# Expert numbers sent later, gates in 8 KB rows, a later residual and 28 lead tiles in a Conformer-S5-PEER block

## The chip, the cores and the metric

The kernel runs on one core of a Trainium2 chip. The metric is the device time of one execution in microseconds; the time before is 3585.42 us, the median of three runs (3583.12 to 3587.71). Engines are named as the profile names them: PE (TensorE, matmuls), PEld (its weight loads), DVE (VectorE), ACT (ScalarE), POOL (GpSimd) and SP (SyncE, which here only issues DMAs).

## The reference

One decoder block over 512 tokens of width 2048, in float32. A convolution branch and a diagonal state-space branch are mixed by gates, projected by `w_out` and added to `x`. The change touches only what follows, the PEER layer:

```python
x = x + merged @ w_out[l]
h = rmsnorm(x, norm_ffn[l])
x = x + peer(h, ...)
return rmsnorm(x, norm_final)

def block(xb):                                   # 128 tokens
    q = (xb @ w_q).reshape(128, 8, 2, 128)
    s = einsum('thcd,hcnd->thcn', q, sub_keys)
    s_top, i_top = top_k(s, 16)                  # per half
    best, pos = top_k(all 256 sums of pairs, 16)
    expert = i_top[..., 0, i] * 128 + i_top[..., 1, j]   # of the pairs that won
    gates = softmax(best)
    act = gelu(einsum('td,thkd->thk', xb, u_tab[expert]))
    return einsum('thk,thkd->td', gates * act, v_tab[expert])
```

There are 128 x 128 = 16384 experts, each with a row of 2048 in `u_tab` and one in `v_tab`; each token uses 8 heads x 16 experts.

## The kernel before

**Three kinds of token.** The last 352 tokens (`ND`) are computed densely: all 16384 experts for all of them, with gates that are zero where an expert is not chosen. The first 128 tokens (block A) and the next 32 (block B) are computed by gathering the rows of the chosen experts by indirect DMAs: 128 rows of U and 128 of V for block A, 32 and 32 for block B (there one partition holds a quarter of a token's experts). A gathered row lands in a `row` tile, three of which exist (`NROW`), and one DVE instruction over 2048 elements takes it in (line 1011 for U, line 1022 for V).

**U tiles and V tiles.** The dense part is cut into 128 tiles of 128 experts. A U tile (`dense_u`, 48 matmuls) multiplies a 128 x 2048 piece of the U table with the normed tokens; GELU on ACT makes `ga` of it (line 862). `weigh` multiplies `ga` by the gates on POOL (line 1081) and splits the product in a high and a low part. A V tile (`dense_v`, 48 matmuls) takes four weighed tiles (a group, `GRP`) and a quarter of the width; its four PSUM results are added into `acc` by DVE (line 1135). There are 32 groups of four V tiles. Every weight piece of 128 x 1024 is loaded by SP (line 222, `wraw`), its high part cast by ACT (`whi`, line 204), its low part made by DVE or by POOL (`wlo`, line 205), because each product is made of three float32r matmuls.

**The lead.** The gates need the whole routing, so the first `LEAD` = 24 U tiles run before any V tile and park their `ga` in DRAM (`d_ga`). For the first `UPOOL` = 10 of them POOL makes both low parts, for the others DVE. After U tile `LAG` - 1 = 5, `transp_routes` makes the softmax (`gt`), spreads the gates of block B over the partitions, and transposes expert numbers and gates. From U tile 6 on, gate steps (`gate_prep`, `gate_tokens`) run between the matmuls: 88 steps of four tokens, each with two comparisons on DVE, a product on POOL (every third step) or ACT, four matmuls and two copies. Every eighth step ends with two DMAs of 1 MB that write `stg` to `d_g`. The last step falls `TAIL` = 2 tiles before the lead's end. From U tile 10 on, `pump_rows` adds `RLEAD` = 1.5 steps of the gathering per tile.

**V-only tiles, then the main loop.** In groups 0 to 4 the next group's four `ga` are reloaded from `d_ga`, so there is no U matmul, only V tiles; one gather step (`RV`) goes with each. `acc` starts as the residual, loaded from `d_x2` by four DMAs in group 0. From then on each iteration has a U tile and a V tile and `rate` gather steps, about 2.9.

**What sets the order.** The kernel is written for a planner, the Tile framework's. It estimates each instruction's duration, and whenever an engine is free by its estimate, that engine gets the instruction that is ready and stands first in the program. Place in the program is thus a priority. The queue that comes out is fixed when the program is built, and on the chip each engine works through its queue in order. `issue_after` (`after` in the code) ties an instruction behind another one on its engine. The gathers are tied behind POOL's latest split or product in that way (`pace`), the softmax's exponential behind the latest GELU. `spread`, which sends the expert numbers or gates of block B to DRAM (line 823) and reads them back in four pieces (line 825), all on POOL, is tied to nothing. Before the change it is called for the expert numbers at line 830, ahead of the first U tile.

Of the kernel before, what the change touches and what calls it, by code (L numbers as in the profile page):

```python
# [7 lines left out]
F32 = mybir.dt.float32  # L8
# [22 lines left out]
G0 = GA + GB  # L31
ND = T - G0
BLKS = [(0, 128), (128, 128), (256, 96)]
NE = 128
LEAD = 24
TAPS = 10
P1 = 2.8
P2 = 4.0
LAG = 6
GM = 1  # L40
TAIL = 2
NR = 18
NROW = 3
RLEAD = 1.5
RV = 1.0
UPOOL = 10
GRP = 4


def _mul(nc, o, a, b):  # L50
    nc.vector.tensor_tensor(o, a, b, op=ALU.mult)
# [6 lines left out]
def _add(nc, o, a, b):  # L58
    nc.vector.tensor_tensor(o, a, b, op=ALU.add)  # L59
# [94 lines left out]
def kernel(ctx, tc, xT, vecs, cst, w_in, conv_w_out, w_vg, w_out, w_q, keysT,  # L154
                      sprm, sb_ch, sb_st, sc_st, gffn, gfin, peer_u, peer_ut, peer_v, peer_vt, out):
    nc = tc.nc
    MS = bass.MemoryType
    const = ctx.enter_context(tc.tile_pool(name="const", bufs=1))
    dram = ctx.enter_context(tc.tile_pool(name="dram", bufs=1, space=MS.DRAM))
# [13 lines left out]
    d_x2 = dram.tile([KD, 128, T], F32, name="d_x2")  # L173
    d_p = dram.tile([4, 64, 64], F32, name="d_p")
    d_k = dram.tile([32, 32, 128], F32, name="d_k")
    d_g = dram.tile([ND // 32, NE // GRP, 128, GRP, 32], F32, name="d_g")
    d_eb = dram.tile([GB, 128], I32, name="d_eb")
    d_gb = dram.tile([GB, 128], F32, name="d_gb")
    d_ga = [dram.tile([128, ND], F32, name=f"d_ga{j}") for j in range(LEAD)]

# [59 lines left out]
    def proj(ps, srcs, ah, al, eng=None, side=0.0, mid=None):  # L240
        for _ in proj_steps(ps, srcs, ah, al, eng, side):
            if mid:
                mid()
# [48 lines left out]
    with tc.issue_after(last_x):  # L292
        for k in range(KD):
            p = k % 3 == 2
# [120 lines left out]
    acc = []  # L415
# [386 lines left out]
    def softmax():  # L802
        g = gt.rearrange("p b h k -> p (b h) k")
        with tc.issue_after(last_ga[0]):
            nc.scalar.activation(g, g, AF.Exp)
        nc.vector.tensor_reduce(zs, g, axis=AX.X, op=ALU.add)
        nc.vector.reciprocal(zs, zs)
        _mul(nc, g, g, zs[:, :, None].to_broadcast([128, TB * 8, 16]))

    eidx = con2.tile([128, HK], I32, name="eidx")  # L810
    eidb = con2.tile([128, GB], I32, name="eidb")
# [3 lines left out]
    def expert_ids(o, b):  # L815
        ef = tmp("ef")[:, :128]
        nc.vector.scalar_tensor_tensor(ef, ij[:, 0, b].rearrange("p h k -> p (h k)"), 128.0,
                                       ij[:, 1, b].rearrange("p h k -> p (h k)"), op0=ALU.mult, op1=ALU.add)
        nc.vector.tensor_copy(o, ef)

    def spread(o, d, src):

        nc.gpsimd.dma_start(d, src[:GB])
        for c in range(REP):
            nc.gpsimd.dma_start(o[c * GB:(c + 1) * GB, :], d[:, c * 32:(c + 1) * 32])

    eid1 = con2.tile([128, HK], I32, name="eid1")
    expert_ids(eidx, 0)
    expert_ids(eid1, 1)
    spread(eidb, d_eb, eid1)  # L830
    _add(nc, sel, ident[:, 0:GB], ident[:, GB:2 * GB])
    for c in range(2, REP):
        _add(nc, sel, sel, ident[:, c * GB:(c + 1) * GB])
# [16 lines left out]
    def row(name):  # L850
        return rowp.tile([128, D], F32, name=name, tag="row", bufs=NROW)
# [6 lines left out]
    def dense_u(j, eng=None, mid=None):  # L858
        pu = pp.tile([128, ND], F32, name="pu", tag="u", bufs=2)
        proj(pu, full(peer_ut, j), h2h, h2l, eng, mid=mid)  # L860
        ga = ring("ga")
        last_ga[0] = nc.scalar.activation(ga, pu, AF.Gelu_apprx_tanh).ins  # L862
        if j < LEAD:
            nc.scalar.dma_start(d_ga[j], ga)
        return ga
# [2 lines left out]

    def transp_routes():
        softmax()  # L870
        spread(gtb, d_gb, gt[:, 1].rearrange("p h k -> p (h k)"))
        for b in range(1, TB):
            lo = max(G0 - b * 128, 0)
            at = b * 128 + lo - G0
            for i, src in enumerate((ij[:, 0, b], ij[:, 1, b], gt[:, b])):
                pt = ps_v()
                nc.tensor.transpose(pt[:, :128], src.rearrange("p h k -> p (h k)"), ident)
                nc.scalar.copy(tT[i][:, at:at + 128 - lo], pt[:, lo:128])

    stg = []  # L880
# [20 lines left out]
    def gate_tokens(t0):  # L901
        if t0 % 32 == 0:
            stg[:] = [gp.tile([128, 64, 32], F32, name="stg", tag="stg", bufs=4) for _ in range(2)]
        oi, oj = hots.pop(t0)
        pg = ps_v((128, 4))
        for t in range(4):
            nc.tensor.matmul(pg[:, :, t], oi[:, t], oj[:, t], start=t == 0, stop=t == 3, skip_group_check=True)
        u0 = t0 % 32
        for q in range(2):
            nc.scalar.copy(stg[q][:, :, u0:u0 + 4], pg[:, q * 64:(q + 1) * 64, :])  # L910
        if u0 == 28:
            for q in range(2):
                nc.sync.dma_start(d_g[t0 // 32, 16 * q:16 * q + 16].rearrange("q i j t -> i q (j t)"),
                                  stg[q].rearrange("p (q j) t -> p q (j t)", j=GRP))

    gars = {}

# [8 lines left out]
    def gate_steps():  # L926
        done[1] += 1
        while done[0] * (LEAD - LAG - TAIL) * KD < steps * done[1] and done[0] < steps:
            if done[0] < steps - 2:
# [111 lines left out]
    steps_g = 2 * HK + 2 * HK // REP + 16  # L1041
    gth = gather()
    gi = [0, 0.0]
# [6 lines left out]

    for j in range(LEAD):
        if j == LEAD - 3:
            gars.update((i, reload(i)) for i in range(GRP))
        dense_u(j, nc.gpsimd if j < UPOOL else None, gate_steps if j >= LAG else None)
        if j == LAG - 1:
            transp_routes()
        if j >= LAG + 4:
            pump_rows(RLEAD)
    gst.close()

# [2 lines left out]
    acc = accp.tile([128, KD, ND], F32, name="acc")  # L1063
# [4 lines left out]
    gq = [None]  # L1068
    last_wh = [None]

    def load_gates(g):
        gq[0] = accp.tile([128, ND // 32, GRP, 32], F32, name="gq", tag="gq", bufs=1)
        nc.gpsimd.dma_start(gq[0].rearrange("p b j t -> p b (j t)"), d_g[:, g].rearrange("b i j t -> i b (j t)"))

    def weigh(j, ga):
        if j == 0:
            load_gates(0)
        if j < LEAD:
            ga = gars.pop(j) if j in gars else reload(j)
        g3 = ga.rearrange("p (b t) -> p b t", t=32)  # L1080
        pace[0] = nc.gpsimd.tensor_tensor(g3, gq[0][:, :, j % GRP, :], g3, op=ALU.mult).ins  # L1081
        wh, wl = ring("wh", F32R), ring("wl", F32R)
        last_wh[0] = split(wh, wl, ga)
        if j % GRP == GRP - 1 and j + 1 < NE:
            load_gates(j // GRP + 1)
# [30 lines left out]

    def dense_v(g, dc, ws):
        pcs = []
        if g == 0:
            nc.sync.dma_start(acc[:, 4 * dc:4 * dc + 4], d_x2[4 * dc:4 * dc + 4, :, G0:].rearrange("k p t -> p k t"))  # L1120
        for p2 in range(GRP // 2):
            with after(last_wh[0]) if g == 0 and dc else nullcontext():
                hi, lo = load_w(peer_vt[g, dc, p2], nc.gpsimd if p2 == 1 else None)
            pcs.append((hi, lo))
        pvs = [ps_v((ND,)) for _ in range(4)]
        for e, i in [(e, i) for e in range(2) for i in range(4)] + [(e, i) for i in range(4) for e in (2, 3)]:
            hi, lo = pcs[e // 2]
            wh, wl = ws[e]
            s = slice(e % 2 * 512 + i * 128, e % 2 * 512 + (i + 1) * 128)
            nc.tensor.matmul(pvs[i], hi[:, s], wh, start=e == 0, stop=False)  # L1130
            nc.tensor.matmul(pvs[i], hi[:, s], wl, start=False, stop=False)  # L1131
            nc.tensor.matmul(pvs[i], lo[:, s], wh, start=False, stop=e == GRP - 1)  # L1132
        for i in range(4):
            a = acc[:, 4 * dc + i]
            _add(nc, a, pvs[i], a)
        if g == NE // GRP - 1:
            turn_out(dc)

    ngrp = NE // GRP
    ws_next = [weigh(j, None) for j in range(GRP)]  # L1140
    rate = (steps_g - gi[0] - RV * LEAD) / (NE - LEAD - 4)
    for g in range(ngrp):
        if g == ngrp - 1:
            for _ in gth:
                pass
            hst.close()
            op = ctx.enter_context(tc.tile_pool(name="op", bufs=1, reuse_waits="tile"))
            tail["ost"] = op.tile([128, len(BLKS), D], F32, name="ost")
            tail["sqs"] = op.tile([128, len(BLKS), 4], F32, name="sqs")
            tail["gfb"] = op.tile([128, D], F32, name="gfb")  # L1150
            nc.gpsimd.dma_start(tail["gfb"], gfin[None, :].to_broadcast([128, D]))
        ws = ws_next
        ws_next = []
        for dc in range(4):
            jn = (g + 1) * GRP + dc
            n = 0 if jn >= NE else rate if jn >= LEAD else RV
            if jn < NE:
                ga = dense_u(jn) if jn >= LEAD else None
                ws_next.append(weigh(jn, ga))
            pump_rows(n / 2)  # L1160
            dense_v(g, dc, ws)
            pump_rows(n / 2)
# [83 lines left out]
```

## Time and profile before

| | us |
|---|---|
| median of the runs (lowest, highest) | 3585.42 (3583.12, 3587.71) |
| the profiled execution | 3586.99 |
| its span, first to last instruction | 3584.8 |
| PE busy in it | 3416.8 |
| DVE busy | 2856.6 |
| POOL busy | 1452.8 |
| ACT busy | 1281.7 |

The profile is that of one execution. Times of instructions are counted from the start of its span. "Waited for" names what ended an idle time. The granted clock (PEclk) is the share of TensorE's full clock of 2.4 GHz.

### The profile page before, as it was taken

The page shows a single profiled execution, that of the slowest core. Times are in us where ns is not written, and L with a number is a line of the kernel's source. Part 1 is how long each engine was busy: PE and PEld are TensorE (multiplying, and loading weights), DVE is VectorE, ACT ScalarE, POOL GpSimd, SP SyncE. Part 2 cuts the span into 40 slices and gives each one's busy share as a digit, 9 for nine tenths or more (in the row PEclk, how much of TensorE's full clock was granted, in tenths as well). Part 3 has the DMA queues.
Part 4 walks back from the last instruction along what each step waited for, and adds up shares of the span by engine and source line. Part 5 has one row for each costly group of instructions (what it writes and reads, how often), then busy time and mean ns, then how long its engine had stood idle before and what let it go on. Part 6 is the DMA issues. An engine that isn't in the chain of part 4 may idle for free. (4 is left out here: it accounts for less than half of the span.)

```text
span 3584.8 us, 50132 instructions
## 1 busy us (share of the span) xinstructions
PE 3416.8 (95%) x19091; PEld 3169.5 (88%) x19091; DVE 2856.6 (80%) x4147; ACT 1281.7 (36%) x2025; POOL 1452.8 (41%) x924
## 2 busy tenths in 40 slices
PE   8999999999999994997889999999999999999998
PEld 6888888888888884986789999999999999999998
DVE  7685848996535997796866999978999898797984
ACT  4234344325223331873223333333333333433333
POOL 1200000110003543343654666656666666465642
PEclk9999999999999997998899999999999999999999
DMA  5533444434444332699877989898989889897882
GB/s 176 154 108 114 129 123 123 140 125 129 135 147 132 113 111 69 188 302 320 273 252 264 357 333 355 340 337 317 356 347 343 335 342 358 285 361 295 344 303 95
DMA packets 261905, 845.30 MB, mean 236 GB/s; under 512 B 42640, under 2 KB 105184, under 8 KB 219904
## 3 DMA queue, kind: packets, MB, share of 16 engines
q1 hardware_dynamic: 189248, 433.25, 35.9%
q0 software_dynamic: 64352, 396.12, 29.4%
q10 hardware_dynamic: 8064, 12.72, 1.0%
q8 instruction: 150, 2.46, 0.3%
q14 instruction: 91, 0.75, 0.1%
HBM read 790.91 MB, written 51.09 MB: 235 GB/s over the span
## 5 line engine op out<-in xcount | busy, mean ns | idle before, releaser
L204 ACT CAST whi<-wraw 128x1024 fp32r<-128x1024 f32 x736 | 771.9, 1051 | 1792.1 <-PE pu L236 610.5
L205 DVE TENSOR_TENSOR wlo<-wraw,whi 128x1024 fp32r<-128x1024 f32 x556 | 743.1, 1351 | 207.6 <-ACT whi L204 206.5
L237 PE MATMUL pu<-h2h,wlo 128*128 128x352 f32 x2048 | 664.9, 325 | 67.7 <-POOL wlo L205 50.6
L1130 PE MATMUL pv<-wh,whi 128*128 128x352 f32 x2048 | 671.1, 328 | 47.8 <-DVE acc L59 29.9
L1132 PE MATMUL pv<-wh,wlo 128*128 128x352 f32 x2048 | 667.5, 326 | 4.7 <-DVE wlo L205 4.7
L235 PE MATMUL pu<-h2l,whi 128*128 128x352 f32 x2048 | 670.1, 327 | 1.1 <-ACT whi L204 1.1
L1131 PE MATMUL pv<-wl,whi 128*128 128x352 f32 x2048 | 667.5, 326 | 0.0
L236 PE MATMUL pu<-h2h,whi 128*128 128x352 f32 x2048 | 660.2, 322 | 0.0
L205 POOL TENSOR_TENSOR wlo<-wraw,whi 128x1024 fp32r<-128x1024 f32 x180 | 446.9, 2484 | 178.0 <-ACT whi L204 169.8
L1011 DVE SCALAR_TENSOR_TENSOR grow<-grow,rows 128x2048 f32<-128x2048 f32 x160 | 421.2, 2635 | 95.0 <-DMA grow<-in_peer_u_dram,eidx 83.3
L1022 DVE SCALAR_TENSOR_TENSOR rows<-grow,act,rows 128x2048 f32<-128x2048 f32 x160 | 427.8, 2674 | 85.1 <-DMA grow<-in_peer_v_dram,eidx 61.7
L237 PEld LDWEIGHTS pu<-h2h,wlo 128*128 128x128 f32 x2048 | 387.9, 189 | 71.9 <-POOL wlo L205 51.1
L1130 PEld LDWEIGHTS pv<-wh,whi 128*128 128x128 f32 x2048 | 390.9, 191 | 52.0 <-DVE acc L59 33.4
L1132 PEld LDWEIGHTS pv<-wh,wlo 128*128 128x128 f32 x2048 | 390.7, 191 | 5.1 <-DVE wlo L205 5.1
L1131 PEld LDWEIGHTS pv<-wl,whi 128*128 128x128 f32 x2048 | 392.4, 192 | 0.0
L235 PEld LDWEIGHTS pu<-h2l,whi 128*128 128x128 f32 x2048 | 386.8, 189 | 2.4 <-ACT whi L204 1.6
L236 PEld LDWEIGHTS pu<-h2h,whi 128*128 128x128 f32 x2048 | 387.7, 189 | 0.0
L235 PE MATMUL ps<-hl,whi 128*128 128x512 f32 x896 | 353.3, 394 | 9.2 <-ACT whi L204 9.2
L237 PE MATMUL ps<-hh,wlo 128*128 128x512 f32 x896 | 350.8, 392 | 0.4 <-DVE wlo L205 0.4
L236 PE MATMUL ps<-hh,whi 128*128 128x512 f32 x896 | 350.5, 391 | 0.0
L1081 POOL TENSOR_TENSOR ga<-gq,ga 128x352 f32<-128x352 f32 x104 | 171.1, 1646 | 434.8 <-ACT ga L862 418.4
L963 POOL DMA_INDIRECT grow<-in_peer_v_dram,eidx x128 | 247.0, 1930 | 76.5 <-DVE rows L1022 41.4
(338 smaller groups left out, 5084.7 us busy)
## 6 DMA issues: line engine op xcount, KB each, us to landing
wraw<-in_peer_ut_dram SPq DMA_DIRECT2D x256, 512.0 KB
wraw<-in_peer_vt_dram SPq DMA_DIRECT2D x256, 512.0 KB
wraw<-in_w_in_dram SPq DMA_DIRECT2D x112, 512.0 KB
d_g<-stg SPq DMA_DIRECT2D x22, 1024.0 KB
gq<-d_g POOLq DMA_DIRECT2D x32, 704.0 KB, 9.3
wraw<-in_w_vg_dram SPq DMA_DIRECT2D x32, 512.0 KB
wraw<-in_w_out_dram SPq DMA_DIRECT2D x32, 512.0 KB
wraw<-in_w_q_dram SPq DMA_DIRECT2D x32, 512.0 KB
```

What stands on the lines that cost most here:

```text
L204: ins = nc.scalar.copy(hi, src).ins
L205: low = (eng or nc.vector).tensor_tensor(lo, src, hi.bitcast(F32), op=ALU.subtract)
L235: nc.tensor.matmul(ps, hi[:, sl], al[k], start=k == 0, stop=False)
L236: nc.tensor.matmul(ps, hi[:, sl], ah[k], start=False, stop=False)
L237: nc.tensor.matmul(ps, lo[:, sl], ah[k], start=False, stop=k == nk - 1)
L963: nc.gpsimd.indirect_dma_start(out=g, out_offset=None, in_=tab, in_offset=bass.IndirectOffsetOnAxis(ap=ids[:, e:e + 1], axis=0))
L1011: nc.vector.scalar_tensor_tensor(g, g, 1.0, x, op0=ALU.mult, op1=ALU.mult, accum_out=act[:, i:i + 1])
L1022: nc.vector.scalar_tensor_tensor(x, g, act[:, i:i + 1], x, op0=ALU.mult, op1=ALU.add)
L1081: pace[0] = nc.gpsimd.tensor_tensor(g3, gq[0][:, :, j % GRP, :], g3, op=ALU.mult).ins
L1130: nc.tensor.matmul(pvs[i], hi[:, s], wh, start=e == 0, stop=False)
L1131: nc.tensor.matmul(pvs[i], hi[:, s], wl, start=False, stop=False)
L1132: nc.tensor.matmul(pvs[i], lo[:, s], wh, start=False, stop=e == GRP - 1)
```

## The change

It has these parts:

- The constants: `LEAD` 24 to 28, `LAG` 6 to 11, `TAIL` 2 to 4, `RLEAD` 1.5 to 2.0, `RV` 1.0 to 1.2. So the gate steps fall into U tiles 11 to 23 instead of 6 to 21, and the V-only tiles become six groups.
- `spread` of the expert numbers is called in `transp_routes`, after U tile 10, instead of ahead of the first U tile.
- `d_g` holds the gates by key first, so that a write from `stg` has rows of 8 KB in place of pieces of 512 B. The read of a group still has pieces of 512 B.
- U tiles from 10 on within the lead have the low part of their second half made by POOL.
- Gather steps in the lead run with U tiles 11 to 24 alone, and none in group 0.
- In group 0 the V results are copied to `acc` by ACT. The residual is loaded in group 4 (`XG`) into a `row` tile, in four pieces, and added by DVE, one add of 1408 elements for each V tile of that group.
- The formula for `rate` follows.

```diff
-LEAD = 24
+LEAD = 28
-LAG = 6
+LAG = 11
-TAIL = 2
+TAIL = 4
-RLEAD = 1.5
-RV = 1.0
+RLEAD = 2.0
+RV = 1.2
+XG = 4
-    d_g = dram.tile([ND // 32, NE // GRP, 128, GRP, 32], F32, name="d_g")
+    d_g = dram.tile([ND // 32, 128, NE // GRP, GRP, 32], F32, name="d_g")
...
     expert_ids(eid1, 1)
-    spread(eidb, d_eb, eid1)
...
     def transp_routes():
         softmax()
+        spread(eidb, d_eb, eid1)
         spread(gtb, d_gb, gt[:, 1].rearrange("p h k -> p (h k)"))
...
-                nc.sync.dma_start(d_g[t0 // 32, 16 * q:16 * q + 16].rearrange("q i j t -> i q (j t)"),
-                                  stg[q].rearrange("p (q j) t -> p q (j t)", j=GRP))
+                nc.sync.dma_start(d_g[t0 // 32, :, 16 * q:16 * q + 16].rearrange("i q j t -> i (q j t)"),
+                                  stg[q].rearrange("p j t -> p (j t)"))
...
-        dense_u(j, nc.gpsimd if j < UPOOL else None, gate_steps if j >= LAG else None)
+        dense_u(j, nc.gpsimd if j < UPOOL else (None, nc.gpsimd), gate_steps if j >= LAG else None)
         if j == LAG - 1:
             transp_routes()
-        if j >= LAG + 4:
+        if LAG <= j < LEAD - 3:
             pump_rows(RLEAD)
...
-        nc.gpsimd.dma_start(gq[0].rearrange("p b j t -> p b (j t)"), d_g[:, g].rearrange("b i j t -> i b (j t)"))
+        nc.gpsimd.dma_start(gq[0].rearrange("p b j t -> p b (j t)"), d_g[:, :, g].rearrange("b i j t -> i b (j t)"))
...
-        if g == 0:
-            nc.sync.dma_start(acc[:, 4 * dc:4 * dc + 4], d_x2[4 * dc:4 * dc + 4, :, G0:].rearrange("k p t -> p k t"))
+        if g == XG:
+            res = row("res")[:, :4 * ND].rearrange("p (k t) -> p k t", k=4)
+            nc.sync.dma_start(res, d_x2[4 * dc:4 * dc + 4, :, G0:].rearrange("k p t -> p k t"))
+            _add(nc, acc[:, 4 * dc:4 * dc + 4], acc[:, 4 * dc:4 * dc + 4], res)
...
-            _add(nc, a, pvs[i], a)
+            if g == 0:
+                nc.scalar.copy(a, pvs[i])
+            else:
+                _add(nc, a, pvs[i], a)
...
-    rate = (steps_g - gi[0] - RV * LEAD) / (NE - LEAD - 4)
+    rate = (steps_g - gi[0] - RV * (LEAD - 8)) / (NE - LEAD - 4)
...
-            n = 0 if jn >= NE else rate if jn >= LEAD else RV
+            n = 0 if jn >= NE else rate if jn >= LEAD else RV if g else 0
```

## Rows read from the trace of the kernel before

**Rows 1.** The page: PE's busy tenths in 40 slices of 89.6 us

```profile
PE   8999999999999994997889999999999999999998
```

**Rows 2.** Stretches: length, then busy us of PE, PEld, DVE, ACT, POOL; clock; DMA share

```profile
1520.40:1651.90 131.50, 121.00 (x843) 118.00 (x842) 123.35 (x146) 95.53 (x263) 60.78 (x33) 0.97 0.94 310
1675.30:1745.30 70.00, 44.58 (x233) 43.41 (x233) 44.66 (x41) 16.26 (x23) 42.80 (x27) 0.80 0.83 289
1745.30:1897.10 151.80, 127.18 (x732) 124.28 (x731) 105.00 (x126) 38.10 (x46) 77.95 (x46) 0.94 0.71 242
1900.00:2300.00 400.00, 400.00 (x2493) 400.00 (x2492) 353.27 (x348) 130.53 (x156) 245.11 (x133) 1.00 0.88 338
```

**Rows 3.** Waits of 1340 to 1450: total us, times, longest

```profile
POOL d_eb L823 <- DVE eid L819: 54.2, 1, 54.2
PE pu L237 <- POOL wlo L205: 48.9, 1, 48.9
DVE zs L806 <- ACT gt L805: 23.6, 1, 23.6
```

**Rows 4.** Timeline of POOL: start, us, instruction, idle before and what ended it

```profile
1347.11 2.45 POOL L205 TENSOR_TENSOR wlo<-wraw,whi 128x1024 fp32r<-128x1024 f32 x1 [1.41 <-ACT whi L204]
1403.73 0.53 POOL L823 DMA_DIRECT2D d_eb<-eid  x1 [54.18 <-DVE eid L819]
1404.27 2.35 POOL L205 TENSOR_TENSOR wlo<-wraw,whi 128x1024 fp32r<-128x1024 f32 x1
```

**Rows 5.** Timeline of SP's DMA issues, 1320 to 1330

```profile
1323.96 0.38 SPq L973 DMA_DIRECT2D xt<-d_x  x1
```

**Rows 6.** Timeline of ACT: the GELU that ends U tiles 3, 5, 9, 10, 29

```profile
1358.37 0.46 ACT L862 ACTIVATE ga<-pu 128x352 f32<-128x352 f32 x1
1424.61 0.46 ACT L862 ACTIVATE ga<-pu 128x352 f32<-128x352 f32 x1
1483.58 0.47 ACT L862 ACTIVATE ga<-pu 128x352 f32<-128x352 f32 x1
1495.30 0.45 ACT L862 ACTIVATE ga<-pu 128x352 f32<-128x352 f32 x1
1982.76 0.45 ACT L862 ACTIVATE ga<-pu 128x352 f32<-128x352 f32 x1
```

**Rows 7.** DVE's groups of 1530 to 1650: busy us, mean ns, idle before

```profile
L892 DVE TENSOR_TENSOR oi<-cs,tT 128x512 f32<-128x512 f32 x44 | 36.5, 830 | 0.2 <-PE pv L907 0.2
L1011 DVE SCALAR_TENSOR_TENSOR grow<-grow,rows 128x2048 f32<-128x2048 f32 x14 | 32.5, 2339 | 3.6 <-DMA grow<-in_peer_u_dram,eidx 3.6
L898 DVE TENSOR_TENSOR oj<-cs,tT 128x512 f32<-128x512 f32 x44 | 29.8, 678 | 0.0
L205 DVE TENSOR_TENSOR wlo<-wraw,whi 128x1024 fp32r<-128x1024 f32 x16 | 23.6, 1475 | 0.0
```

**Rows 8.** Timelines of DVE and of POOL around 1820

```profile
1816.06 0.52 DVE L205 TENSOR_TENSOR wl<-gar,wh 128x352 fp32r<-128x352 f32 x1
1818.96 4.27 DVE L205 TENSOR_TENSOR wl<-gar,wh 128x352 fp32r<-128x352 f32 x1 [0.49 <-ACT wh L204]
1819.56 2.41 POOL L205 TENSOR_TENSOR wlo<-wraw,whi 128x1024 fp32r<-128x1024 f32 x1
```

**Rows 9.** PE's waits, 1650 to 1750 and 1745 to 1897; DVE's rows, 1745 to 1897

```profile
PE pv L1130 <- ACT wh L204: 10.6, 1, 10.6
...
PE pv L1130 <- DVE acc L59: 24.6, 10, 5.2
...
L1011 DVE SCALAR_TENSOR_TENSOR grow<-grow,rows 128x2048 f32<-128x2048 f32 x15 | 36.9, 2457 | 24.1 <-DMA grow<-in_peer_u_dram,eidx 24.1
```

**Rows 10.** The DMAs of stg (issue ns min/median/max); the x2 load on the chain

```profile
L913 SPq DMA_DIRECT2D d_g<-stg x22: 377/1074/12087, 1449.9 to 1653.7; - x22
...
2376.58 11.73 DMA xt<-d_x
```

**Rows 11.** The loads of gq: issue to landing

```profile
DMA to landing us min/median/max: 7.5/9.3/11.0
```

## The prediction

> **What bounds the kernel now.** First the page: TensorE (PE) is 9 tenths busy or more in nearly every slice, with one deep hole at slice 16 and a shallow trough two to four slices later [rows 1]. So only time in which PE stands still can be won, and it lies between 1358 and 1900 us; behind that PE has no gap (400.00 of 400.00 us busy from 1900 to 2300) [rows 2]. Next the waits, to see what ends each loss.
>
> *The hole.* The lead runs "U tiles", 48 matmuls each; 2493 matmuls in 400 us make 7.70 us per tile [rows 2]. The fourth ends at 1358.37, the sixth at 1424.61: 66.2 us for two tiles, 50.8 too many [rows 6]. POOL waited 54.18 us to send the expert numbers of block B (d_eb) until DVE had made them at 1403, and the split of the next U tile stands behind that DMA [rows 3, 4].
>
> *The gate stretch.* From 1520.4 to 1651.9 nine U tiles with gate steps take 14.6 us each; DVE is busy 123.35 of 131.5 us, PE 121.00 at a granted clock of 0.97, nearly its upper level of 2.4 GHz [rows 2]. DVE bounds it.
>
> *Hand-over and V-only tiles.* The first four V tiles take 70.0 us instead of 30.8; the longest wait, 10.6 us, is for the first weighed gates [rows 2, 9]. The next sixteen take 151.8 us, 9.49 each: PE waits for DVE's adds (24.6 us), and DVE itself stood 24.1 us waiting for gathered rows [rows 2, 9].
>
> **The change, part by part.** I follow PE from the end of U tile 5 (1424.61) to the state "28 U and 24 V tiles done". The kernel before reaches it so: U tile 29 ends at 1982.76 with 25 V tiles done, that is three tiles more, 1982.76 - 23.1 = 1959.7 [rows 6]. What follows is the same matmuls in both.
>
> *Expert numbers sent later: 0.* Moving the call moves the DMA's place in the program, and so its priority, not its place in POOL's queue. The planner gives a free engine whatever is ready by its own estimate. The load of xt shows how far that reaches: the program has it behind the eleventh U tile, yet SP issued it at 1323.96, before the first ended [rows 5]. POOL has room as well: before each split it stood 1.41 us waiting for ACT [rows 4]. The numbers depend on nothing in between, so the planner, which thinks them ready where it does now, will put the DMA into the gap before the next split. The four reads of d_eb and POOL's wait stay where they are. If that is wrong, 50.8 us go: the first rival.
>
> *LAG 11: +38.5 us of gate-free tiles ahead, neutral for PE, but DVE idles.* Five more U tiles run before the softmax: 5 x 7.70 = 38.5, to 1463.1. DVE already stood 23.6 us before the softmax [rows 3]; now it stands some 62.
>
> *Gates in 13 tiles instead of 16, 2 rows per tile instead of 1.5, the second weight half on POOL.* Steps per tile go from 90/16 = 5.6 to 90/13 = 6.9. Start-up: tiles 6 to 9 took 1483.58 - 1424.61 = 59.0, against 4 x 11.72 (tile 10: 1495.30 - 1483.58), so 12 us [rows 6]. PE alone needs 7.70 + 6.9 x (11.72 - 7.70)/5.6 = 12.6 per tile. DVE needed 123.35/9 = 13.7; add 1.3 steps at (36.5 + 29.8)/44 = 1.51 us, 1.9; add half a row at 2.34, 1.2; take off one split at 1.48: 15.3 [rows 2, 7]. POOL's split in its place does not come free: a DVE subtraction that took 0.52 us alone took 4.27 beside a POOL split of 2.41 and the product behind it [rows 8]. So between 0 and 2.4 us come back to DVE; I take 1.4, since the row shows a full block, but POOL will sometimes find DVE waiting. 16.7, times 131.5/123.35 for DVE's waits, is 17.8 (16.3 to 18.9). Rows start in the third tile, so: 12 + 2 x 12.6 + 3 (the row norm) + 11 x 17.8 = 236, to 1699.
>
> The Trainium skill, page "SBUF — State Buffer", section "Who interferes with whom", says that a DVE instruction with two SBUF inputs and a GpSimd instruction that reads SBUF exclude each other for the whole of the instruction. By that rule each moved split would block DVE for all of its 2.4 us and the end would come some 12 us later than forecast. The 4.27 us row agrees with it.
>
> *LEAD 28, TAIL 4.* Four U tiles without gates: 30.8, to 1730. In that time the last gates are written and read. *8 KB rows*: SP issues the 22 writes in a median of 1.07 us, at worst 12.09 [rows 10]; that queue carries the weights too, but PE's waits of the gate stretch fall to DVE, so 0 there and the gain is in the hand-over. The gates are read back in the same 512-byte pieces, now 16 KB apart; that load lands in 9.3 us [rows 11]. I take 0: it is asked for a tile or more ahead. Bounds: -24 (22 x 1.07, all the SP time gained) to +47 (each of the five loads of the V-only tiles late by its whole 9.3 us).
>
> *No rows in group 0, its sums copied by ACT, no load of x2 at the start.* The 39.2 us lost in the first four V tiles were waits for gates and for splits [rows 9]; I leave 4: 35, to 1765 (bounds 31 to 70). The 16 copies fall to ACT, busy 38.1 of 151.8 us among V-only tiles [rows 2]: 0; were ACT full, 16 of the GELU's 0.46 us [rows 6], 7 us.
>
> *RV 1.2.* A V tile with one row costs 9.49 - 7.70 = 1.79 beyond PE's time; 1.2 rows cost 2.15, 9.85 per tile. Sixteen tiles of groups 1 to 3 and 5: 158.
>
> *The residual in group 4.* Each of its four V tiles takes one of the three row buffers for x2, and DVE adds 1408 elements per partition: an estimate from the 2048-element row, 1408/2048 x 2.34 = 1.6 us. A x2 load of 1 MB landed in 11.73 us [rows 10], and DVE takes its work in order, so I add a wait as one more row has it, 1.8: 13.2 per tile, 53 (bounds: 39, all hidden, to 86, four times 9.85 + 11.73, nothing hidden). To 1976, 16 us behind 1959.7.
>
> *Later.* The rest of the rows, 336 - 28 - 24 over 96 tiles, is 2.96 per tile instead of 2.91; DVE's 353 of 400 us hold that [rows 2]. 0.
>
> **The sum.** The profiled execution took 3586.99 us with a span of 3584.8, 1.6 above the median of the runs. So 3587 + 16 = 3603 beside that execution, and 3601 against the median of 3585.42, slower by 0.4%.
>
> **The rivals.**
> *First, the other side, faster: the DMA does go behind the eleventh tile's splits.* Then POOL never waits and the 50.8 us go; the same sum ends at 3601 - 51 = 3550. For it: DVE makes the numbers at 1403, and the eleventh tile would begin at 1358.4 + 6 x 7.70 = 1405, so nothing would stand. Against it: xt's place [rows 5]. It decides at one point, POOL's order at 1350 us.
> *Second, slower still: the row buffers' turn-round bounds the V-only tiles.* In sixteen tiles with sixteen rows each row took 9.49 us [rows 2]. If it is the row that takes that and not the tile, 24 rows and 4 x2 loads take 28 x 9.49 = 266 instead of 211: 3656. Against it: later 2.9 rows pass in 15.4 us without a loss on PE.
> *Third: POOL's split is free for DVE and the hand-over is won whole.* 11 x 1.5 + 4 + 14 (x2 hidden) less: 3566 at best. I count that into the forecast's own range.
>
> **Chances.** The forecast 0.62, with its own range 3566 to 3625; the first rival 0.22; the second 0.16. About 0.2% (7 us) is what a measurement of this kernel tells from no change. Of the forecast's 0.62, 0.36 are slower by more, 0.14 within, 0.12 faster. Together: faster 0.34, same 0.14, slower 0.52. The range reaches down over the first rival with the same spread, and up to 3635.
>
> **What would show it.** In the trace after: whether POOL's wait for the expert numbers is still some 54 us and PE's gap 49. Whether U tiles 13 to 23 take near 17.8 us with DVE at over 90%, or 12.6 with PE at 100%. Whether the first V tile follows the last U tile by under 12 us. Whether the x2 tiles of group 4 show DVE waiting for their DMA. The prediction is wrong if the hole is gone, or if the gate stretch runs at PE's pace.

## The result, and the profile after

The changed kernel takes 3623.8 us (median of four runs, 3621.4 to 3626.5) against 3586.6 us for the kernel before in the same session: a ratio of 1.0104 (95% interval 1.0087 to 1.0122), 37.2 us slower. The profiled execution took 3623.7 us with a span of 3621.9.

PE's tenths on the page, to be read beside [rows 1]: the hole at slice 16 is still there, and the trough behind it holds six slices under 9 tenths instead of three.

```profile
PE   8999999999999994888788999999999999999998
```

The waits of 1340 to 1450 (total us, times, longest) and POOL's timeline (start, us, instruction, idle before and what ended it) show why. They answer to [rows 3, 4].

```profile
POOL d_eb L824 <- DVE eid L820: 54.2, 1, 54.2
...
PE pu L238 <- POOL wlo L206: 48.8, 1, 48.8
DVE wlo L206 <- ACT whi L205: 44.0, 1, 44.0
```

```profile
1347.73 2.40 POOL L206 TENSOR_TENSOR wlo<-wraw,whi 128x1024 fp32r<-128x1024 f32 x1 [1.45 <-ACT whi L205]
1404.33 0.53 POOL L824 DMA_DIRECT2D d_eb<-eid  x1 [54.20 <-DVE eid L820]
1404.88 2.35 POOL L206 TENSOR_TENSOR wlo<-wraw,whi 128x1024 fp32r<-128x1024 f32 x1
```

The DMA of the expert numbers is called eleven U tiles later in the program and stands at the same place in POOL's queue: POOL waits 54.20 us for it, as it waited 54.18. New is DVE's idle stretch of 44.0 us behind the hole: with LAG 11 there are no gates to make yet.

The GELU rows that end U tiles 5, 10, 23, 27 and 29 [rows 6] and the stretches between them (length, then busy us of PE, PEld, DVE, ACT and POOL; granted clock, DMA share, GB/s), beside [rows 2]. The windows are tiles 6 to 10, tiles 14 to 23, tiles 24 to 27, the first four V tiles, groups 1 to 3, group 4, group 5, and a piece of the main loop.

```profile
1424.90 0.45 ACT L862 ACTIVATE ga<-pu 128x352 f32<-128x352 f32 x1
...
1463.29 0.46 ACT L862 ACTIVATE ga<-pu 128x352 f32<-128x352 f32 x1
...
1702.06 0.46 ACT L862 ACTIVATE ga<-pu 128x352 f32<-128x352 f32 x1
...
1739.76 0.46 ACT L862 ACTIVATE ga<-pu 128x352 f32<-128x352 f32 x1 [5.45 <-PE pu L238]
...
2013.97 0.46 ACT L862 ACTIVATE ga<-pu 128x352 f32<-128x352 f32 x1
```

```profile
1424.90:1463.30 38.40, 38.40 (x243) 38.38 (x242) 2.45 (x2) 12.31 (x17) 19.16 (x8) 1.00 0.51 160
1516.00:1702.10 186.10, 153.79 (x1028) 150.21 (x1028) 181.57 (x186) 117.07 (x346) 99.09 (x55) 0.92 0.75 274
1702.10:1739.80 37.70, 32.09 (x187) 30.93 (x185) 16.16 (x12) 8.89 (x13) 19.32 (x13) 0.95 1.00 372
1739.80:1786.30 46.50, 34.55 (x205) 33.39 (x206) 18.19 (x19) 20.98 (x37) 22.32 (x14) 0.96 0.63 207
1786.30:1913.40 127.10, 103.50 (x576) 99.42 (x575) 93.27 (x101) 31.31 (x39) 71.29 (x45) 0.93 0.78 271
1913.40:1953.70 40.30, 34.45 (x200) 33.29 (x199) 35.57 (x39) 9.64 (x11) 24.84 (x14) 0.96 0.84 292
1953.70:1990.10 36.40, 30.80 (x179) 29.93 (x178) 25.55 (x32) 8.25 (x11) 15.45 (x9) 0.95 0.72 242
2000.00:2400.00 400.00, 399.69 (x2486) 398.90 (x2485) 359.55 (x353) 129.70 (x155) 255.18 (x134) 1.00 0.90 340
```

The state "28 U and 24 V tiles" comes at 2013.97 - 23.1 = 1990.9 us (the end of tile 29, less two U tiles and one V tile at 7.70), 31 behind the 1959.7 of before. Six more are lost after it: the last U tile's GELU comes 36.8 us later than before (3562.4 for 3525.6).

The 22 writes of gates now take SP a third of a microsecond each to issue (min/median/max in ns), against 377/1074/12087 [rows 10]:

```profile
L914 SPq DMA_DIRECT2D d_g<-stg x22: 320/344/569, 1487.9 to 1701.1; - x22
```

### The profile page after: what moved, and what is told of

It reads as the page before. It is cut to its first block, busy times and chain, and to the rows that moved or that the text cites. A ratio compares the mean times of both kernels' runs of the same rounds, so it can differ in the third digit from the quotient of the medians.

```text
span 3621.9 us, 50123 instructions
## 1 busy us (share of the span) xinstructions
PE 3431.8 (95%) x19091; PEld 3178.1 (88%) x19091; DVE 2850.0 (79%) x4117; ACT 1287.9 (36%) x2041; POOL 1480.7 (41%) x942
## 5 line engine op out<-in xcount | busy, mean ns | idle before, releaser
L206 DVE TENSOR_TENSOR wlo<-wraw,whi 128x1024 fp32r<-128x1024 f32 x538 | 715.1, 1343 | 263.7 <-ACT whi L205 260.5
L206 POOL TENSOR_TENSOR wlo<-wraw,whi 128x1024 fp32r<-128x1024 f32 x198 | 490.0, 2476 | 215.1 <-ACT whi L205 207.3
L1012 DVE SCALAR_TENSOR_TENSOR grow<-grow,rows 128x2048 f32<-128x2048 f32 x160 | 431.4, 2697 | 108.5 <-DMA grow<-in_peer_u_dram,eidx 91.8
L1082 POOL TENSOR_TENSOR ga<-gq,ga 128x352 f32<-128x352 f32 x100 | 158.7, 1587 | 422.8 <-ACT ga L862 418.4
```

Of the source, the lines that this page charges most:

```text
L206: low = (eng or nc.vector).tensor_tensor(lo, src, hi.bitcast(F32), op=ALU.subtract)
L1012: nc.vector.scalar_tensor_tensor(g, g, 1.0, x, op0=ALU.mult, op1=ALU.mult, accum_out=act[:, i:i + 1])
```

## The experiments

Each is timed beside the kernel before in the same session (medians 3583 to 3586 us); the ratio to it has its 95% interval. By these intervals two of the kernels below can be told apart when they differ by some 7 or 8 us, with the most runs by 5. "The changed kernel" is the 3623.8 of above. The labels e1 to e16 name the kernels in the text behind.

**1. The hole, and what it was good for (e1).** A tie in place of a mere move:

```diff
-        spread(eidb, d_eb, eid1)
+        with after(pace[0]):
+            spread(eidb, d_eb, eid1)
```

> The changed kernel with one thing more: the DMA that sends the expert numbers (and its four reads) is tied behind POOL's second split of U tile 10, so that the planner can't put it ahead. Theory (the planner, not the program's place, put that DMA at 1350 us, and POOL's wait for it is the whole hole): POOL's wait of 54 us and PE's gap of 49 us go, the gate stretch keeps its length, and the time is 3623.8 - 51 = 3573 us. Rival (the hole only moves, to DVE's routing or the softmax, which the gates need anyway): PE stands before U tile 11 instead, with DVE busy on the routing, and less than 25 us are won: over 3599 us.

Measured: 3591.2 us (3588.0 to 3597.1), 1.0021 [1.0012, 1.0030]. The DMA went where it was sent and the hole at 1358 is gone, but 32.6 us came back, not 51: between theory and rival. The waits of this kernel from 1340 to 1450 name a new hole, 18 us, at U tile 10:

```profile
PE pu L238 <- DVE wlo L206: 18.3, 1, 18.3
POOL d_eb L824 <- DVE eid L820: 18.1, 1, 18.1
```

DVE now makes the expert numbers at 1420 instead of 1404, and tile 10's low part stands behind them. What holds DVE up shows in two groups of its work between 1349 and 1403 (shapes, count, busy us, mean ns), first this kernel, then the changed one:

```profile
L794 DVE TENSOR_TENSOR oh<-pf,cs 128x512 f32<-128x512 f32 x7 | 12.9, 1863 | 0.0
L797 DVE TENSOR_TENSOR oh<-oh,if 128x512 f32<-128x512 f32 x8 | 9.7, 1228 | 0.0
L799 DVE TENSOR_REDUCE ij<-oh 128x32 f32<-128x512 f32 x8 | 5.2, 668 | 0.0
```

```profile
L797 DVE TENSOR_TENSOR oh<-oh,if 128x512 f32<-128x512 f32 x12 | 7.9, 683 | 0.0
L799 DVE TENSOR_REDUCE ij<-oh 128x32 f32<-128x512 f32 x12 | 7.9, 676 | 0.0
L794 DVE TENSOR_TENSOR oh<-pf,cs 128x512 f32<-128x512 f32 x11 | 7.3, 685 | 0.0
```

The same comparison (line 794 of the changed kernel) takes 1.86 us on average instead of 0.69 and the product behind it (line 797) 1.23 instead of 0.68, while the reduction, with one input, keeps its 0.67. At the changed kernel's means the two groups would have taken 10.3 us instead of 22.6: 12 of the 16 us by which the numbers come later. In this kernel POOL makes a split every 3.8 us here (32.45 us busy of the 54); in the changed one it stands in the hole (1.13 us busy). So the hole had kept POOL out of DVE's way, and without it POOL's splits for the next U tiles delay the routing that PE waits for after them. No run takes these splits off POOL, so this rests on the durations.

**2. LAG (e2, e3).** Back to 6, with and without the hole (the second has the DMA tied behind POOL's work of U tile 10):

```diff
-LAG = 11
+LAG = 6
-        if LAG <= j < LEAD - 3:
+        if 11 <= j < LEAD - 3:
```

and in the second kernel the call leaves `transp_routes` for the loop over lead tiles:

```diff
+        if j == 10:
+            with after(pace[0]):
+                spread(eidb, d_eb, eid1)
```

> The changed kernel with LAG 6 again (gate steps in U tiles 6 to 23, 18 tiles; rows stay in tiles 11 to 24; the hole stays). Theory (the gate stretch is bound by DVE's work, and LAG 11 leaves DVE idle for 36 of the 38.4 us before it while the hole already gives DVE its time): the same DVE work starts 38 us earlier, U tile 23 ends some 35 us earlier, 3589 us. Rival (the stretch is bound by PE's clock and by waits of its own tiles, not by DVE's sum): the five more gate tiles cost PE as much as they take off the others, under 12 us are won, 3612 us or more.

> The changed kernel with LAG 6 and with the expert numbers' DMA tied behind POOL's work of U tile 10. Theory: without the hole U tile 10 would end at 1412, and DVE has the numbers at 1403, so LAG 6 and LAG 11 give DVE nearly the same start; 0 to 9 us less than the changed kernel with the tie alone, 3564 to 3573 us. Rival (LAG 11 costs its 35 us whatever the hole does): 3538 us. Other rival (at LAG 6 the gate matmuls in PE's queue wait for a softmax that isn't there yet, and a new hole opens): 3580 us or more.

Measured: 3616.2 us (3608.3 to 3622.2), 1.0083 [1.0069, 1.0097] with the hole, and 3601.8 us (3592.5 to 3606.9), 1.0043 [1.0029, 1.0057] without it. So where the hole stays, LAG 6 is 7.7 us faster by the medians, far less than the theory's 35 and no more than can just be told from no change. Where the hole is gone it loses 10.6: there PE's queue has the transposes of the routing ahead of U tile 6, and PE stands 31 us until DVE has made their input:

```profile
PE pv L877 <- DVE ij L799: 34.5, 2, 31.2
```

In the first kernel U tile 23 ends 12.5 us earlier, and tiles 24 to 27 take 46.7 us, 9 more than in the changed kernel: most of what the stretch wins is lost behind it.

**3. POOL's half of the splits (e4).**

```diff
-        dense_u(j, nc.gpsimd if j < UPOOL else (None, nc.gpsimd), gate_steps if j >= LAG else None)
+        dense_u(j, nc.gpsimd if j < UPOOL else None, gate_steps if j >= LAG else None)
```

> The changed kernel with both low parts of U tiles 10 to 27 made by DVE, as the kernel before had it from tile 10 on. Theory (POOL's split holds DVE up by about what it takes off it, 1.4 of 1.48 us): the gate stretch keeps its 18.7 us per tile, 3617 to 3631 us. Rival (POOL's split costs DVE nothing): 13 splits of 1.48 us come back to DVE, 3643 us. Other rival (POOL's split blocks DVE for its whole 2.4 us): 12 us are won, 3612 us.

Measured: 3608.3 us (3605.4 to 3610.5), 1.0065 [1.0052, 1.0079]: 15.5 us won, the third answer and a little more (its edit moves back the splits of U tiles 10 to 27, 18 in all). DVE's groups in the ten tiles 14 to 23 (and the end of tile 13), first with the splits on DVE (170.5 us), then as changed (186.5 us):

```profile
L893 DVE TENSOR_TENSOR oi<-cs,tT 128x512 f32<-128x512 f32 x67 | 56.0, 835 | 3.2 <-PE pv L908 3.2
...
L899 DVE TENSOR_TENSOR oj<-cs,tT 128x512 f32<-128x512 f32 x67 | 45.4, 678 | 0.0
L206 DVE TENSOR_TENSOR wlo<-wraw,whi 128x1024 fp32r<-128x1024 f32 x22 | 29.1, 1328 | 0.0
```

```profile
L893 DVE TENSOR_TENSOR oi<-cs,tT 128x512 f32<-128x512 f32 x66 | 72.4, 1097 | 1.9 <-POOL oi L895 0.9 <-PE pv L908 0.9
...
L899 DVE TENSOR_TENSOR oj<-cs,tT 128x512 f32<-128x512 f32 x67 | 51.5, 768 | 0.0
L206 DVE TENSOR_TENSOR wlo<-wraw,whi 128x1024 fp32r<-128x1024 f32 x11 | 15.6, 1415 | 0.0
```

POOL's eleven splits in the changed kernel:

```profile
L206 POOL TENSOR_TENSOR wlo<-wraw,whi 128x1024 fp32r<-128x1024 f32 x11 | 28.3, 2577 | 0.2
```

Eleven splits taken off DVE save it 29.1 - 15.6 = 13.5 us and cost it 16.4 + 6.1 = 22.5 in longer comparisons. DVE "busy" is not all DVE at work: the time by which it is held up stands inside the instruction's own duration (1097 ns for 835).

**4. Tie and DVE's splits together (e5)**, the edits of 1 and 3.

> The changed kernel with two things at once: the expert numbers' DMA tied behind POOL's second split of U tile 10, and both low parts of U tiles 10 to 27 made by DVE. The tie alone gave 3591.2, DVE's splits alone 3608.3. Theory (the gate stretch is bound by DVE's work plus POOL's blocking, wherever it starts): both gains add, 3591 - 15 = 3576 us, under the kernel before. Rival (what the tie left over, PE's wait for DVE's low part at U tile 10, grows when both low parts wait for DVE): 3585 us or more.

Measured: 3578.0 us (3572.4 to 3587.1), 0.9985 [0.9976, 0.9994]. The two add.

**5. The late residual (e6), and the pieces of 512 B (e7)**, each put back as before in the changed kernel (their hunks of the change reversed):

> The changed kernel with the residual as before: acc loaded from d_x2 in group 0, all sums by DVE, nothing in group 4. Theory (the copies cost since ACT works in order and has the gates' splits, which wait for reloads, ahead of them): PE's waits of 9.6 us for the copies go, and group 4 loses its adds (4 x 1.6 us): 5 to 12 us less, 3612 to 3619 us. Rival (the reloads' late landing is what costs, whoever empties the PSUM): same within 5 us, 3619 to 3629. Other rival (the four x2 loads push the V weights back in SP's queue, as the kernel before had it): 3634 us or more.

> The changed kernel with d_g as before: writes and reads in pieces of 512 B. Theory (SP's issue time beside PE's stretch is hidden): 3617 to 3631 us, no change, although the issue of the 22 writes goes from a median of 0.34 us back to some 1.1. Rival (the small pieces burden the DMA engines, which the rows, the weights and the gates' read share at the hand-over): 3634 us or more.

Measured: 3627.0 us (3622.7 to 3629.2), 1.0125 [1.0109, 1.0140], and 3623.2 us (3621.7 to 3633.2), 1.0121 [1.0104, 1.0137]. Neither moves the time beyond what can be told from no change. The theory on the copies falls; the issue of the writes goes back to a median of 0.78 us. POOL's first read of the gates then waits 10.6 us for the last of these writes, where in the changed kernel it waits 8.3 for a `ga` on its way to `d_ga`; the time does not show it.

**6. Eight rows fewer in the lead (e8)**, and the gates' products of group 0 tied behind POOL's splits (e9):

```diff
-        if LAG <= j < LEAD - 3:
+        if LAG <= j < 21:
```
```diff
-        pace[0] = nc.gpsimd.tensor_tensor(g3, gq[0][:, :, j % GRP, :], g3, op=ALU.mult).ins
+        with after(pace[0]) if j < GRP else nullcontext():
+            pace[0] = nc.gpsimd.tensor_tensor(g3, gq[0][:, :, j % GRP, :], g3, op=ALU.mult).ins
```

> The changed kernel with gather rows in U tiles 11 to 20 alone (20 steps in the lead instead of 28; the other 8 fall to the main loop, whose rate goes up by 0.08 per tile). Theory (a row costs DVE 2.5 us in the gate stretch, and the rows of tiles 22 to 24 also hold up the splits of tiles 24 to 27 and the hand-over): U tile 23 ends 15 us earlier, tiles 24 to 27 take 31 us instead of 37.7, the first four V tiles 42 instead of 46.5, and the main loop gives 6 to 9 us back: 3603 to 3608 us. Rival (tiles 24 to 27 are held by the weights' loads beside the gates' last writes, not by rows): they keep 37 us, 3612 us or more.

> The changed kernel with the gates' products of group 0 (weigh) tied behind POOL's latest split, so that POOL makes the low parts of U tiles 26 and 27 before it waits for the gates' read. Theory (in the four gate-free U tiles POOL's queue stands at the gates' read, and the next split behind it): tiles 24 to 27 take 33 us instead of 37.7 and the hand-over is no longer, 3617 to 3620 us. Rival (these tiles are held by loads: the DMA engines are full from 1702 to 1740 and the weights come late): they keep 37 us, 3621 to 3627.

Measured: 3623.4 us (3622.4 to 3636.7), 1.0122 [1.0105, 1.0139], and 3621.9 us (3616.6 to 3625.4), 1.0099 [1.0084, 1.0115]. Both theories fall on the total. Without its rows U tile 23 ends 9.6 us earlier, but tiles 24 to 27 still take 38.6 us, and what is left of the gain, 7.2 us at U tile 28, is gone by the last U tile. POOL's timeline in tiles 24 to 27 of this kernel:

```profile
1702.32 1.18 POOL L1074 DMA_DIRECT2D gq<-d_g  x1 [3.50 <-DMA wraw<-in_peer_ut_dram]
1712.36 2.67 POOL L1082 TENSOR_TENSOR gar<-gq,gar 128x352 f32<-128x352 f32 x3 [8.86 <-DMA gq<-d_g]
1714.98 2.33 POOL L206 TENSOR_TENSOR wlo<-wraw,whi 128x1024 fp32r<-128x1024 f32 x1
```

POOL waits 8.86 us for the gates' read with the next U tile's split behind it, and PE waits 6.4 us for that split. With the products tied behind the splits the four tiles take 33.4 us instead of 37.7, as forecast, although the DMA engines are as full as before (share 1.01), and the next U tile (28) still ends 4 us later than in the changed kernel: the gain is lost at the hand-over.

**7. The same cure on the faster kernel (e10)**, and the rest of the change left out (e11: the kernel before, LAG 11, the tied DMA). e10 has the edits of 1, the tied products of 6, and the first line here; e11 is the kernel before with the rest:

```diff
+        dense_u(j, nc.gpsimd if j < UPOOL or j >= 24 else None, gate_steps if j >= LAG else None)
```
```diff
-LAG = 6
+LAG = 11
-    spread(eidb, d_eb, eid1)
...
+        with after(pace[0]):
+            spread(eidb, d_eb, eid1)
         spread(gtb, d_gb, gt[:, 1].rearrange("p h k -> p (h k)"))
...
-        if j >= LAG + 4:
+        if j >= 10:
```

> The kernel with the tied expert numbers and DVE's splits (3578.0), but U tiles 24 to 27 have both low parts made by POOL, and the first group's products are tied behind these splits. There PE waited 9.8 us for DVE's low part, because DVE stood 9.1 us at a row that hadn't landed. Theory (in-order queues at the hand-over): that wait goes, 3567 to 3571 us. Rival (DMA engines full at the hand-over, the weights and the first gates late in any case): 3575 us or more.

> The kernel before with two parts of the change only: LAG 11, and the expert numbers sent after U tile 10, here tied behind POOL's latest split. 24 lead tiles, TAIL 2, 1.5 rows per lead tile, the residual and the pieces of 512 B stay as before. Theory (the stretch up to the V tiles is bound by DVE, which then starts on the gates some 20 us earlier; the other parts of the change are worth nothing or less): U tile 23 ends near 1645 instead of 1675.8, 3555 to 3565 us, less than the 3578 of the whole change with the same tie and DVE's splits. Rival (28 lead tiles, the earlier end of the gates and the late residual are what shortens the hand-over): what is won is lost there, 3578 us or more.

Measured: 3579.2 us (3572.7 to 3584.5), 0.9982 [0.9973, 0.9991], no gain: the theory falls. And 3565.5 us (3557.6 to 3569.2), 0.9945 [0.9931, 0.9958]: two parts of the change, LAG 11 and the later call, with the tie that the change lacks, make the kernel before faster than both kernels, and than the repaired whole change (e5) by 12.5 us.

**8. Which other part costs the 12.5 us.** Four lead tiles and the gates' end first; rows among V-only tiles second; then the rows' placing alone, put into the fast kernel (e15) and taken out of the slow one (e16). e12 is experiment 4 with `LEAD = 24` and `TAIL = 2`, e13 is e11 with `RV = 0.0`, and e15 is e11 with

```diff
-RLEAD = 1.5
-RV = 1.0
+RLEAD = 2.0
+RV = 1.2
-        if j >= 10:
+        if LAG <= j < LEAD - 3:
-    rate = (steps_g - gi[0] - RV * LEAD) / (NE - LEAD - 4)
+    rate = (steps_g - gi[0] - RV * (LEAD - 8)) / (NE - LEAD - 4)
-            n = 0 if jn >= NE else rate if jn >= LEAD else RV
+            n = 0 if jn >= NE else rate if jn >= LEAD else RV if g else 0
```

e16 is e12 with the same lines the other way round.

> The changed kernel with the tie and DVE's splits (3578.0), and LEAD 24 and TAIL 2 as before; the residual in group 4, ACT's copies, no rows in group 0, the 8 KB rows, 2 rows per lead tile (20 in all) and LAG 11 stay. Theory (four more lead tiles and the earlier end of the gates cost the 13 us: four more V-only tiles, and a stretch of U tiles that starves on full DMA engines): 3563 to 3568 us, as the kernel before with the tie and LAG 11. Rival (the late residual with its copies and adds is what costs): 3575 us or more.

> The kernel before with the tie and LAG 11 (3565.5), and no gather rows in the 20 V-only tiles after the first four nor in these (RV 0): 24 rows go to the main loop, 3.15 per tile instead of 2.91. Theory (a row among V-only tiles costs 1.8 us, since DVE works in order and stands waiting for it to land; one in the main loop costs 0.9): 24 x 0.9 = 22 us less, 3541 to 3550 us. Rival (V-only tiles are bound by the adds and the reloads, not by rows, or the main loop becomes DVE's at 92% busy): 3560 us or more.

> The kernel before with the tie and LAG 11 (3565.5) and the change's placing of the rows alone: 2 per tile in U tiles 11 to 20, none in group 0, 1.2 per V-only tile after that: 39 steps ahead of the main loop instead of 45. Theory (a row left to the main loop costs some 2 us there and is not won back ahead of it): 3574 to 3580 us. Rival (the residual, ACT's copies or the 8 KB rows make the 13 us): 3562 to 3569 us.

> The changed kernel with tie, DVE's splits, LEAD 24 and TAIL 2 (3579.7), and the placing of the rows as before: 1.5 per tile in U tiles 10 to 23, 1 per V-only tile from group 0 on: 45 steps ahead of the main loop. Theory (rows): 3562 to 3569 us. Rival (residual, copies, 8 KB rows): 3576 us or more.

Measured: e12 3579.7 us (3573.9 to 3585.8), 0.9985 [0.9977, 0.9994], the rival's time: with this placing of the rows, LEAD 28 and TAIL 4 cost nothing (e5 has 52 row steps ahead of the main loop, e12 39). That the residual and its copies are what costs, as the rival has it, is refuted by e16, which keeps them. e13 3563.2 us (3553.7 to 3572.2), 0.9929 [0.9915, 0.9943]: the theory falls. Its V-only stretch is 36 us shorter (U tile 23 to 24: 191.0 us, against 227.2 in e11), 1.5 per row moved, and its main loop from U tile 28 to 127 is 44 us longer (1596.6, against 1553.0; the profiled execution is e13's slowest). e15 3576.2 us (3571.2 to 3588.7), 0.9985 [0.9974, 0.9995]; e16 3560.4 us (3558.6 to 3567.7), 0.9931 [0.9918, 0.9944]. The two swap places as the theory said: by the medians the placing of the rows costs 11 us (e15 against e11) and 19 (e12 against e16).

The theory's reason does not hold, though. e13 leaves 24 more steps to the main loop and is no slower in all; and e15, with six more steps left, in the profiles wins 5.1 us up to U tile 28 and loses 6.0 from there to U tile 97. Most of the difference comes after that, in U tiles 98 to 103, where the gathering of block A ends and that of block B begins. These six tiles in e11 and in e15 (length, then busy us of PE, PEld, DVE, ACT and POOL; granted clock, DMA share, GB/s), and PE's wait in them that e11 does not have:

```profile
3021.50:3119.80 98.30, 96.26 (x593) 95.66 (x592) 83.61 (x83) 41.14 (x51) 51.62 (x31) 0.98 0.82 296
3022.40:3127.20 104.80, 96.42 (x595) 95.59 (x594) 89.09 (x90) 41.45 (x52) 52.00 (x32) 0.97 0.84 304
```

```profile
PE pv L1133 <- DVE wlo L205: 6.6, 1, 6.6
```

They take 99.1 us in the kernel before and 97.7 in e16, but 106.0 in e12 and 102.9 in the changed kernel, where the same wait is 7.5 and 5.7 us. That is 6 of the 8.6 us by which the last U tile ends later in e15's profile than in e11's, and 8 of the 10.1 between e12's and e16's. So what costs is mainly where in the tiles block B's start falls, and seven more DVE instructions fall into these tiles in e15 than in e11 (90 for 83).

**9. No gate product on POOL (e14)**, in the kernel of e11:

```diff
-GM = 1
+GM = 0
```

> The kernel before with the tie and LAG 11 (3565.5), and the gate products that POOL makes (every third step) made by ACT instead. Theory (POOL's product blocks DVE's comparison beside it, some 0.44 us a time, and ACT has room at two thirds busy): 29 x 0.44 = 13 us less at most, 3553 to 3560 us. Rival (ACT becomes what the gate stretch waits for, since it also makes the high parts, four scalings per step and the copies to stg): 3566 us or more.

Measured: 3548.1 us (3542.7 to 3554.1), 0.9890 [0.9876, 0.9904], the fastest of all: 17 us won, more than the theory gave. DVE's groups in the gate stretch, first e11 (1516 to 1660), then this (1516 to 1646):

```profile
L893 DVE TENSOR_TENSOR oi<-cs,tT 128x512 f32<-128x512 f32 x51 | 43.5, 852 | 1.4 <-PE pv L908 1.4
L1012 DVE SCALAR_TENSOR_TENSOR grow<-grow,rows 128x2048 f32<-128x2048 f32 x15 | 37.5, 2509 | 2.6 <-DMA grow<-in_peer_u_dram,eidx 2.6
...
L205 DVE TENSOR_TENSOR wlo<-wraw,whi 128x1024 fp32r<-128x1024 f32 x18 | 24.3, 1355 | 7.4 <-ACT whi L204 7.4
```

```profile
L893 DVE TENSOR_TENSOR oi<-cs,tT 128x512 f32<-128x512 f32 x51 | 35.1, 688 | 0.0
L1012 DVE SCALAR_TENSOR_TENSOR grow<-grow,rows 128x2048 f32<-128x2048 f32 x15 | 34.2, 2288 | 0.0
L205 DVE TENSOR_TENSOR wlo<-wraw,whi 128x1024 fp32r<-128x1024 f32 x18 | 21.9, 1222 | 9.7 <-ACT whi L204 9.7
```

With POOL doing nothing but DMA issues beside it, these three groups have the shortest means of any stretch shown here (688, 2288 and 1222 ns). Together they take 14.1 us less, and U tile 23 ends 14.6 us earlier (1644.8 for 1659.4).

## Why the direction of the prediction was right and its size wrong

The direction held, and so did the ground for it: slower, since the hole stays. The size did not: 16 us forecast, 37 measured. The step that failed is the hand-over, two terms of the sum: "Four U tiles without gates: 30.8" measured 37.7 us, and the first four V tiles, "I leave 4: 35", measured 46.5. That is 18.4 of the 21 us that the forecast was short; the other errors nearly cancel. The prediction took the 39.2 us lost in the first four V tiles of the kernel before for waits that the change removes, all but 4, though its rows show a wait of 10.6 [rows 9]; 15.7 stayed (46.5 - 30.8). In the four U tiles the order in POOL's queue makes 4.3 of the 6.9 us too many (e9). What makes the loss in the V tiles is open: the waits name late reloads, and no run shows it. Step by step:

- **Expert numbers: 0.** Right, and as the reason given would have it: the place in POOL's queue did not move. That the DMA's place in that queue makes the hole at 1358 is shown by e1, which moves it. The price of the first rival was wrong, though: without the hole 32.6 us come back and not 50.8, since a second hole of 18 us opens where DVE makes the numbers later.
- **LAG 11: neutral.** The five tiles ended at 1463.29, forecast 1463.1. Undoing it beside the hole gives 7.7 us (e2), hardly to be told from nothing; without the hole LAG 11 is the better by 10.6 (e3).
- **Gate stretch: 236.** 238.8 us (1702.06 - 1463.29), in part by luck. Tiles 11 to 13 took 52.3 us for 58.0 forecast, tiles 14 to 23 18.6 each for 17.8. In these ten tiles two terms erred in opposite ways. With both splits on DVE the prediction's own terms make (15.3 + 1.48) x 131.5/123.35 = 17.9 per tile, and e4 took 17.05. POOL's split, which the forecast had nearly even (1.4 for 1.48), costs 15.5 us by the medians of e4, whose ten tiles are 16 us shorter: by the row of 4.27 us [rows 8] it should have been priced at its whole 2.4. The Trainium skill, "SBUF — State Buffer", section "Who interferes with whom", spoke against the forecast here: it says that a DVE instruction with two SBUF inputs and a GpSimd instruction that reads SBUF exclude each other. The estimate of 12 us that the prediction worked out by that rule comes nearer to e4's 15.5 than the forecast does. The same section says that a DVE instruction with at most one SBUF input, outside DVE's two-port modes, does not contend with GpSimd. The trace of e1 agrees: the reduction with one input kept its 668 ns beside POOL's splits.
- **Four U tiles without gates: 30.8.** 37.7 us (+6.9). They were costed as PE time alone; but here the gates are written and read back, V weights are fetched, rows land, and the DMA engines are full (share 1.00). With the gates' products moved behind the splits (e9) the four tiles take 33.4 us, with the DMA engines as full, so 4.3 of the 6.9 us are POOL's queue. The waits from 1702 to 1740 show weights and rows landing late, and POOL standing ahead of the gates' read:

```profile
ACT whi L205 <- DMA wraw<-in_peer_ut_dram: 16.0, 3, 11.5
DVE grow L1012 <- DMA grow<-in_peer_u_dram,eidx: 12.5, 4, 4.7
POOL gq L1074 <- DMA d_ga<-ga: 8.3, 1, 8.3
```

- **First four V tiles: 35.** 46.5 us (+11.5). By the waits from 1740 to 1786, the reloads land late, POOL's product waits for them, ACT's split for POOL, and PE for ACT's copies behind it:

```profile
POOL gar L1082 <- DMA gar<-d_ga: 14.3, 2, 7.8
...
PE pv L1133 <- ACT acc L1139: 9.6, 3, 6.2
```

  That the copies themselves are the cause is refuted by e6. The rest of the chain is read from the waits and not shown. From U tile 23's GELU to the last sum of the fourth V tile, the eleven kernels with 28 lead tiles (the changed one, e1 to e10) take 81 to 94 us, for 66 forecast: none of their edits removes the loss.
- **V-only tiles.** A V tile of groups 1 to 3 took 10.6 us instead of 9.85, one of group 5 9.1, and one of group 4 with the residual 10.1 instead of 13.2: the x2 loads were hidden. Together 203.8 us for 211: 9 us more in groups 1 to 3 and 16 less in groups 4 and 5, so these errors nearly cancel.
- **Later: 0.** 5.7 us between U tiles 28 and 127, 3.8 of them in U tiles 98 to 103, where block B begins (102.9 us for 99.1). The prediction asked only whether DVE's 353 of 400 us busy [rows 2] hold 2.96 rows per tile; where the schedule of the rows puts block B's start did not enter. e15 and e16 show what that schedule is worth altogether, 11 to 19 us. Why one start is dearer than another stays open, beyond PE's wait there for DVE's low part.

At "28 U and 24 V tiles" the errors are 2.8 + 6.9 + 11.5 - 7.2 = 14 of the 15 us by which 1990.9 misses 1976; the main loop adds 6. Of the parts undone one at a time, two are clear of noise: POOL's splits, 15.5 us, and the placing of the rows, 11 and 19, measured in kernels without the hole. LAG's 7.7 is not, and the other parts give nothing that can be measured; LEAD 28 was undone only together with row steps. That these figures add up to about the 37.2 measured can be chance: that parts in different kernels add is not shown, and LAG's own effect turns its sign with the hole.

The second rival (a row's turn-round, 3656) did not come: V-only tiles ran at 9.1 to 10.6. The third, POOL's split free for DVE, is the opposite of what e4 shows.

## What to carry to other kernels

A later place in the program moved nothing here (POOL's wait was 54.18 us and then 54.20), because a planner that fills queues by readiness decides the order: check the engine's queue, and tie the instruction to one behind which it shall stand. Work handed from a busy DVE to POOL can cost DVE more than it takes off it: 13.5 us were saved, and the comparisons beside POOL's 28.3 us of splits lengthened by 22.5. Look for one group with two mean durations in two stretches. Work that can be placed anywhere (here the rows) is not free where an engine seems 10% idle: 24 rows taken out of the V-only tiles saved 36 us there and cost 44 in the main loop (e13). Measure both places, and the place where one phase of the work gives way to the next.

## What the runs showed that was not expected

A stall can protect: the hole of 49 us on PE kept POOL quiet for 54 us, and without it DVE's routing ended 16 us later (1420 for 1404). And a third of the gate products, 30 with a median of 1.36 us, cost 17 us more of the whole time on POOL than on ACT (e14), though ACT was then busy 114.8 of 130 us in the gate stretch.
